# A gated recurrent layer: the order of three engines written out, and the side sums moved to other products

## The chip, the cores and the metric

The kernel runs on one core of one Trainium2 chip. The metric is the time of one execution on the device in microseconds (us), here the median of three runs. A core has a matrix engine (TensorE, PE in the profile, its weight loads PEld), an engine for elementwise work (VectorE, DVE), one for functions and copies (ScalarE, ACT), GpSimd (POOL), and a queue engine (SyncE, SP) that issues most DMAs. Each engine works through its own instructions in order and waits for others by semaphores.

## The reference

Two post-norm decoder layers on a sequence of 1024 positions and width 1024, in float32: a dilated attention layer with an MLP, then a gated recurrent layer (HGRN2, eight heads of 128) with an MLP. The change is in the recurrent layer:

```python
q_raw, f_raw, i_raw = jnp.split(x @ w_in, [H * K, 2 * H * K], axis=-1)
log_f = jnp.logaddexp(jnp.log(lb), jnp.log1p(-lb) + jax.nn.log_sigmoid(z))
key = (1.0 - lb) * jax.nn.sigmoid(-z)          # z is f_raw
q = jax.nn.silu(q_raw)
b = jnp.cumsum(log_f, axis=3)                  # within chunks of 64
a = jnp.where(causal, einsum(q * exp(b), key * exp(-b)), 0.0)
kv = einsum(key * exp(b_last - b), v)
state = exp(b_last) * state + kv               # from chunk to chunk
o = a @ v + (q * exp(b)) @ state_before
o = o * rsqrt(mean(o * o) + eps) * norm_g
y = o @ w_out
...
return jnp.square(jax.nn.relu(x @ w_up)) @ w_down     # the MLP
```

## The kernel before

**Products.** Large products are cut into 2 x 2 blocks and made with seven block products instead of eight (numbers 1 to 7 in the code, in an order such as 1, 6, 2, 7, 5, 4, 3). Each operand is split into a high and a low half (`split`: a ScalarE copy, then a VectorE subtraction), and a block product of the gated layer is 4 x 3 = 12 matmuls of 128 x 512. Several block products of one tile add up in one PSUM bank, so the next may start only when the bank has been copied or added out.

**Side sums.** Four of the seven products need sums of weight blocks. For the gated layer they are made ahead, by a generator (`Gates.sums`) that is advanced one step at a time beside the MLP of layer 0. A step is one VectorE instruction on 128 x 512, in half of the steps with a ScalarE copy behind it. GpSimd's queue writes the results to DRAM (`gwd`), and SyncE's loads them back as `H`. There are twelve units of eight steps. In the up-projection `SIDE_UP` gives steps per product, in the down-projection `SIDE_DOWN` steps per step by number of product, and the rest runs in the gated layer.

**The gated layer** (`hgrn`). A table `gw.seq` lists the block products: 28 for the values (`values`, bank tiles "pvx" and "pvy"), seven gate products for each head (`gate`, tile "pg"; numbers 1, 2, 6, 3 give z and the forget gate, 5, 7, 4 the query). Then each head has small pieces: `forget` and `query` (ScalarE functions Abs, Exp, Ln with VectorE passes between), transposes of the keys ("hpt" to "k2n"), products of keys and values ("kvps"), the running states ("stA", "stB", fifteen VectorE updates), the product of queries and keys ("as", masked into "aT"), the outputs ("ho"), their squares and scaling ("sq", "rms", "on") and the transposes back ("opt" to "oN"). In the kernel before, `head_pieces` gives them as seven lists, one of which is emitted after each gate product. The order in which an engine takes them is then left to the scheduler.

**The out-projection** (`outproj_ln`, tile "pmm") begins with three tiles over six heads. `pre` loads and splits the first `NPRE` heads' rows before it. Pieces of the last heads are emitted between its matmuls.

`in_order` ties the instructions of the engines it is given to the order in which they are written, by dependences without a semaphore. The up-projection uses it for TensorE, VectorE and SyncE; the gated layer did not use it.

## Time and profile before

| | |
|---|---|
| median of 3 runs | 2710.69 us (2709.29 to 2713.7) |
| the profiled execution | 2713.53 us, granted TensorE clock 0.996 |
| its span | 2711.8 us |
| value products, first to last | 1659.9 to 1775.6 us |
| gate products, first to last | 1694.4 to 1978.6 us |
| out-projection of the gated layer | 1986.8 to 2089.5 us |

The span runs from the first to the last instruction. A row of a group of instructions names the source line, the engine, the operation, the tile written and the tiles read, the shape and the count; behind the bar stand busy time, mean ns of one, then the idle time of the engine before them and what ended it. A busy TensorE is a union of overlapping matmuls, so its real pace is read from the count of matmuls in a window.

### The profile page before, as it was taken

To read this page: it belongs to the slowest core of one execution; us is meant where nothing else is said; L and a number is where in the kernel's file an instruction comes from. 1 tells how busy PE (TensorE), PEld (TensorE's weight loads), DVE (VectorE), ACT (ScalarE), POOL (GpSimd) and SP (SyncE) were. 2 spreads that over 40 slices of the span, in tenths; PEclk is the share of its full clock that TensorE was granted. 3 is DMA by queue.
4 is the path that set the end of the run, shared out by engine and by line. 5 is a ranking of instruction groups with operands and counts; after the bars stand their busy time and mean duration, and the time that the engine had idled before them with its cause. 6 is when DMAs were issued, how large, how long until landed. Compare 5 with 4: busy or idle time off the path is not lost.

```text
span 2711.8 us, 41759 instructions
## 1 busy us (share of the span) xinstructions
PE 2654.8 (98%) x14600; PEld 2171.6 (80%) x14600; DVE 2109.3 (78%) x4053; ACT 1420.0 (52%) x3169; POOL 216.5 (8%) x424
## 2 busy tenths in 40 slices
PE   8999999999999999999999999999989999999998
PEld 6888888888887778877788887777778888888887
DVE  7768878778788788888787988557778786678686
ACT  5556555555655626445553546446653644444443
POOL 1021222212132100000000000000000000000000
PEclk9999999999999999999999999999999999999999
DMA  8677778777789634577895962754443464486653
GB/s 326 211 243 227 225 205 238 225 229 230 242 263 308 206 98 174 204 251 270 304 337 163 370 212 86 258 195 138 154 131 121 153 224 159 162 298 235 225 181 122
DMA packets 240899, 583.30 MB, mean 215 GB/s; under 512 B 29488, under 2 KB 51248, under 8 KB 240688
## 3 DMA queue, kind: packets, MB, share of 16 engines
q1 hardware_dynamic: 213584, 503.06, 54.6%
q0 software_dynamic: 27104, 77.58, 9.4%
q8 instruction: 115, 1.88, 0.3%
q14 instruction: 96, 0.79, 0.1%
HBM read 429.44 MB, written 125.89 MB: 205 GB/s over the span
## 4 chain that ended last, share of the span: by engine, by line
PE 82%; DVE 8%; ACT 4%; DMA 3%; issue 2%; SPq 0%; DVEq 0%; POOL 0%; ACTq 0%
PE pmm L816 8%; PE pmm L818 7%; PE pmm L817 7%; PE pup L1369 6%; PE pup L1371 6%; PE pup L1370 6%; PE pdy L1519 4%; PE pdy L1520 4%; PE pdy L1516 4%; PE pdx L1519 3%; PE pdx L1520 3%; PE pdx L1516 3%; PE pmm L217 2%; PE o L691 2%; PE pmm L218 2%
## 5 line engine op out<-in xcount | busy, mean ns | idle before, releaser
L816 PE MATMUL pmm<-xh,H 128*128 128x512 f32 x1008 | 403.2, 400 | 8.1 <-ACT H L522 6.4
L818 PE MATMUL pmm<-xh,H 128*128 128x512 f32 x1008 | 395.8, 393 | 4.2 <-DVE H L531 4.0
L817 PE MATMUL pmm<-xl,H 128*128 128x512 f32 x1008 | 395.3, 392 | 4.0 <-DVE xl L172 4.0
L816 PEld LDWEIGHTS pmm<-xh,H 128*128 128x128 f32 x1008 | 190.7, 189 | 57.4 <-issue 8.6
L818 PEld LDWEIGHTS pmm<-xh,H 128*128 128x128 f32 x1008 | 190.6, 189 | 46.9 <-DVE H L531 5.9
L817 PEld LDWEIGHTS pmm<-xl,H 128*128 128x128 f32 x1008 | 190.8, 189 | 42.2 <-DVE xl L172 4.6
L1516 PE MATMUL pdy<-dT,dS 128*128 128x512 f32 x512 | 199.2, 389 | 0.0
L1519 PE MATMUL pdy<-dT,dS 128*128 128x512 f32 x512 | 199.2, 389 | 0.0
L1520 PE MATMUL pdy<-dT,dS 128*128 128x512 f32 x512 | 199.2, 389 | 0.0
L171 ACT ACTIVATE dS<-dr 128x512 fp32r<-128x512 f32 x192 | 119.2, 621 | 56.1 <-PE pdy L1520 23.8
L172 DVE TENSOR_TENSOR dS<-dr,dS 128x512 fp32r<-128x512 f32 x192 | 131.1, 683 | 16.4 <-ACT dS L171 15.8
L630 ACT ACTIVATE p<-p,stats 128x256 f32<-128x256 f32 (+1 forms) x256 | 118.2, 465 | 48.9 <-DVE stats L627 48.3
L627 DVE CUSTOM_DVE_ANT_0 p<-s,mask 128x256 f32<-128x256 f32 (+1 forms) x256 | 82.4, 376 | 47.5 <-PE s L599 47.5
L171 ACT ACTIVATE dT<-dr 128x512 fp32r<-128x512 f32 x128 | 79.2, 624 | 71.9 <-DVE dr L1489 38.3
L1330 ACT ACTIVATE H<-wc 128x512 fp32r<-128x512 f32 x128 | 77.5, 624 | 73.9 <-DVE wc L1323 40.6
L1516 PEld LDWEIGHTS pdy<-dT,dS 128*128 128x128 f32 x512 | 96.1, 188 | 20.0
L1519 PEld LDWEIGHTS pdy<-dT,dS 128*128 128x128 f32 x512 | 96.1, 188 | 20.0
L1520 PEld LDWEIGHTS pdy<-dT,dS 128*128 128x128 f32 x512 | 96.1, 188 | 19.8
L891 POOL DMA_DIRECT2D rot<-e x176 | 85.8, 493 | 281.6 <-ACT e L849 62.2
L1519 PE MATMUL pdx<-dT,dS 128*128 128x512 f32 x256 | 99.7, 389 | 0.7 <-DVE dT L172 0.7
L1520 PE MATMUL pdx<-dT,dS 128*128 128x512 f32 x256 | 99.4, 389 | 0.0
L1516 PE MATMUL pdx<-dT,dS 128*128 128x512 f32 x256 | 98.4, 389 | 0.0
(534 smaller groups left out, 7040.2 us busy)
## 6 DMA issues: line engine op xcount, KB each, us to landing
xh<-xtd SPq DMA_DIRECT2D x116, 512.0 KB, 6.9
xl<-xtd SPq DMA_DIRECT2D x116, 512.0 KB, 5.8
dr<-hd SPq DMA_DIRECT2D x192, 256.0 KB, 5.0
dr<-in_w_down_dram SPq DMA_DIRECT2D x160, 256.0 KB, 5.3
wa<-in_w_up_dram SPq DMA_DIRECT2D x48, 512.0 KB, 3.9
gwd<-pH POOLq DMA_DIRECT2D x48, 512.0 KB, 6.5
H<-gwd SPq DMA_DIRECT2D x48, 512.0 KB, 5.5
rot<-e POOLq DMA_DIRECT2D x176, 128.0 KB, 6.4
```

Source lines behind the costliest of these rows:

```text
L171: act(hi, raw, AF.Copy)
L172: nc.vector.tensor_sub(lo, raw, hi.bitcast(F32))
L630: act(p[:, h], p[:, h], AF.Exp, bias=self.sS[:, 0, h, b:b + 1], scale=-1.0, accum_out=self.sS[:, 1, h, b:b + 1])
L816: nc.tensor.matmul(o, wh, hi[k // 2][:, c], start=begin and k == 0, stop=False, skip_group_check=True)
L817: nc.tensor.matmul(o, wh, lo[k // 2][:, c], start=False, stop=False, skip_group_check=True)
L818: nc.tensor.matmul(o, wl, hi[k // 2][:, c], start=False, stop=end and k == 3, skip_group_check=True)
L1369: nc.tensor.matmul(o, wh, xf.h(b, k), start=begin and k == 0, stop=False, skip_group_check=True)
L1370: nc.tensor.matmul(o, wh, xf.l(b, k), start=False, stop=False, skip_group_check=True)
L1371: nc.tensor.matmul(o, wl, xf.h(b, k), start=False, stop=end and k == 3, skip_group_check=True)
L1516: nc.tensor.matmul(o[q], h, T_[:, L], start=begin, stop=False, skip_group_check=True)
L1519: nc.tensor.matmul(o[q], h, T_[:, R], start=False, stop=False, skip_group_check=True)
L1520: nc.tensor.matmul(o[q], l, T_[:, L], start=False, stop=end, skip_group_check=True)
```

## The change

The pieces of a head become fifteen methods of a class `Head`, and a table puts each of them behind a numbered product: the pieces of head h begin at `first[h] + 3`, beside its own gate products, and end at `first[h] + 15`, in the second head after it. Everything in the layer is written inside `in_order` for TensorE, VectorE and ScalarE.

```diff
-        heads = {}
+        first = {h: gw.seq.index(("g", h, 1)) for h in range(1, 8)}
+        first[0] = first[1] - 7
...
+        for h in range(8):
+            w = Head(h)
+            s0 = first[h]
+            g, q = (...) if h == 0 else (s0 + 3, s0 + 6)
+            for n, f in enumerate((w.forget0, w.forget1, w.forget2, w.forget3)):
+                at(g + n, f)
+            at(q, w.query0)
+            at(g + 3, w.forget4)
+            at(q + 1, w.query1)
+            at(s0 + 7, w.values)
+            at(s0 + 8, w.trans)
+            at(q + 2, w.query2)
+            at(s0 + 9, w.kv)
+            at(s0 + 9, lambda w=w: w.states(0))
+            at(s0 + 10, lambda w=w: w.states(1))
+            at(s0 + 10, w.amat)
+            at(s0 + 11, w.masked)
+            at(s0 + 12, w.omats)
+            at(s0 + 13, w.squares)
+            at(s0 + 14, w.scaled)
+            at(s0 + 15, w.outs)
+        rank = {"scaled": 0, "outs": 2}
+        order = in_order((mybir.EngineType.PE, mybir.EngineType.DVE, mybir.EngineType.Activation))
...
+            for f in sorted(fill.pop(n, []), key=lambda f: rank.get(f.__name__, 1)):
+                f()
+            for k in range(n + 2, n + 6):
+                if k < len(gw.seq) and k <= n + gw.lead(k):
+                    gw.split(k)
+            if 15 < n < first[1] or n >= first[1] and (n - first[1]) % 7 in (0, 2, 6):
+                next(gw.side, None)
+            k = n - first[7]
+            if 0 <= k < 3:
+                pre(oN, k, 0)
+            if 3 <= k + 0 < 6:
+                pre(oN, k - 3, 1)
```

The values' products change places with gate products, the sums get other places, one more head's rows are split ahead of the out-projection, and banks change: "as" goes to the bank "o", "opt" to "o" and "s", which "kvps" and "ho" use too.

```diff
-NPRE = 2
+NPRE = 3
-SIDE_UP = (0.25, 0.96)
-SIDE_DOWN = {5: 0.9, 4: 0.25, 2: 0.25}
+SIDE_UP = {(1, 2): 2, (1, 7): 1, (1, 5): 2, (2, 2): 2, (2, 7): 1, (2, 5): 2}
+SIDE_DOWN = {5: 0.95, 4: 0.4, 2: 0.3}
...
-            self.seq = v[0] + v[1] + [("g", h, i) for h, i in ((0, 2), (0, 1), (1, 2), (2, 2), (0, 5), (0, 6), (0, 3), (0, 7))]
-            self.seq += v[2][:1] + [("g", 0, 4)] + v[2][1:] + v[3] + v[4] + v[5] + v[6]
+            self.seq = v[0] + [("g", 0, 2), ("g", 1, 2)] + v[1]
+            self.seq += [("g", h, i) for h, i in ((0, 1), (2, 2), (0, 5), (0, 6), (0, 3), (0, 7))]
+            self.seq += v[2] + [("g", 0, 4)] + v[3] + v[4] + v[5] + v[6]
...
-            t = self.raw[e] = wp.tile([P, 512], F32, name="wr", tag="p")
+            t = self.raw[e] = U("wr")[:, 0:512] if 3 < n < 16 else wp.tile([P, 512], F32, name="wr", tag="p")
...
+        def lead(self, k):
+            e = self.seq[k]
+            return 0 if e is None else {1: 5, 2: 4, 4: 5}.get(e[2], 0) if e[0] == "g" and k > 20 else 2
...
-                a = bank("s", "as")
+                a = self.am = bank("o", "as")
...
-                pt = bank("pt", "opt")
+                    pt = bank("s" if j else "o", "opt")
```

In heads 6 and 7 the sixth product of a head (number 2 of the head after next) does not exist; the table then holds `None` there, and the slot has no matmuls.

What the change moves is best seen on three places. The first is ScalarE in the middle of the heads. Before, from the squares "sq" of one head to the Exp of "ze" of the next; "a_..." are the tiles a1 and a3 of the forget gate and the query, "qe" and "ze" the query and z:

```order
L1946 ACTIVATE sq,rms<-ho 128x128 x6
L2090 ACTIVATE dec<-a_18192 128x16
L1946 ACTIVATE sq,rms<-ho 128x128 x2
L2055 ACTIVATE ze<-pg 128x512
L2085 ACTIVATE ls<-ze,hc_C 128x1024
L1948 ACTIVATE rms<-rms 128x8
L1949 ACTIVATE rms<-rms 128x8
L2067 ACTIVATE qe<-pg 128x512
L2088 ACTIVATE ze<-ze,hc_C 128x1024
```

And ScalarE there now:

```order
L2120 ACTIVATE qe<-pg 128x512
L2005 ACTIVATE sq,rms<-ho 128x128 x8
L2007 ACTIVATE rms<-rms 128x8
L2008 ACTIVATE rms<-rms 128x8
L1916 ACTIVATE ls<-ze,hc_C 128x1024
L1918 ACTIVATE dec<-a_18477 128x16
L1925 ACTIVATE a_18589<-qe 128x1024
L1928 ACTIVATE ze<-ze,hc_C 128x1024
L1932 ACTIVATE a_18589<-a_18589 128x1024
L1933 ACTIVATE a_18589<-a_18589,one 128x1024
L2112 ACTIVATE qe<-pg 128x512
L1948 ACTIVATE k2n<-hpt 128x512 x2
```

The copy of the head's last gate product ("qe<-pg") stood behind the squares and stands ahead of them now; the Exp of "ze", on which the transposes "hpt" wait, follows the squares and the Abs of the query.

The second is VectorE from the scaled outputs "on" to the first states, at the same place of a head. Before:

```order
L1956 TENSOR_TENSOR on<-ho,rms 128x512 x2
L2057 TENSOR_TENSOR ze<-pg,ze 128x512
L2099 SCALAR_TENSOR_TENSOR a_18048<-qe,a_18048 128x1024
L2100 TENSOR_TENSOR a_18048<-a_18048,a_17911 128x1024
L2102 TENSOR_TENSOR qe<-qe,a_18048 128x1024
L1915 COPY stA<-kvps 128x128
```

Now, with a step of the side sums ("pH<-ps,pH") and two splits of gate weights ("H<-wr,H") between them:

```order
L2110 TENSOR_TENSOR ze<-pg,ze 128x512
L2012 TENSOR_TENSOR rms<-rms 128x8
L2013 TENSOR_TENSOR rms<-rms 128x8
L2014 TENSOR_SCALAR rms<-rms 128x8
L2015 TENSOR_TENSOR rms<-rms 128x8
L2019 TENSOR_TENSOR on<-ho,rms 128x512 x2
L1934 SCALAR_TENSOR_TENSOR a_18016<-qe,a_18016 128x1024
L1935 TENSOR_TENSOR a_18016<-a_18016,a_17902 128x1024
L1801 TENSOR_TENSOR pH<-ps,pH 128x512
L1939 TENSOR_TENSOR qe<-qe,a_18016 128x1024
L171 TENSOR_TENSOR H<-wr,H 128x512 x2
L1976 COPY stA<-kvps 128x128
```

The addition "ze<-pg,ze" moved ahead of the scaling, and three more instructions stand ahead of the states.

The third is VectorE in the up-projection of layer 0, from one product 6 ("upb<-pup,upa") to product 5 of the same pair. The sums' steps are the rows with "ps" and "pH". Before:

```order
L1384 TENSOR_TENSOR upb<-pup,upa 128x512
L1338 TENSOR_TENSOR H<-wc_12407,H 128x512
L1411 TENSOR_TENSOR upb<-upc,upa 128x512
L1796 TENSOR_TENSOR pH<-ps,pH 128x512
L1338 TENSOR_TENSOR H<-wc_12357,H 128x512
L1411 TENSOR_TENSOR upa<-upb 128x512
L1804 TENSOR_TENSOR ps<-pa,pb 128x512
L1387 TENSOR_TENSOR upc<-pup,upa 128x512
L1338 TENSOR_TENSOR H<-wb,H 128x512
L1808 TENSOR_TENSOR ps<-ps,pa 128x512
L1393 TENSOR_TENSOR upc<-pup,upc 128x512
```

And now:

```order
L1389 TENSOR_TENSOR upb<-pup,upa 128x512
L1343 TENSOR_TENSOR H<-wc_12363,H 128x512
L1416 TENSOR_TENSOR upb<-upc,upa 128x512
L1343 TENSOR_TENSOR H<-wc_12318,H 128x512
L1416 TENSOR_TENSOR upa<-upb 128x512
L1813 TENSOR_TENSOR ps<-ps,pa 128x512
L1801 TENSOR_TENSOR pH<-ps,pH 128x512
L1392 TENSOR_TENSOR upc<-pup,upa 128x512
L1343 TENSOR_TENSOR H<-wb,H 128x512
L1821 TENSOR_TENSOR ps<-pa 128x512
L1398 TENSOR_TENSOR upc<-pup,upc 128x512
```

The step beside product 6 is gone; beside product 2 there are two.

## The prediction

> **What bounds the kernel now.** The page comes first: the span, the busy shares and the chain of waits.

> ```profile
> span 2711.8 us, 41759 instructions
> PE 2654.8 (98%) x14600; PEld 2171.6 (80%) x14600; DVE 2109.3 (78%) x4053; ACT 1420.0 (52%) x3169; POOL 216.5 (8%) x424
> PE 82%; DVE 8%; ACT 4%; DMA 3%; issue 2%; SPq 0%; DVEq 0%; POOL 0%; ACTq 0%
> ```

> TensorE sets the time: it is idle for 2711.8 - 2654.8 = 57 us, and the change gives it the same products to do. So the change can only move TensorE's waits, and I look for them by stage, in the view of windows (columns: window, its length, then busy us and count of PE, PEld, DVE, ACT, POOL; granted TensorE clock; DMA). The first two windows hold the same 1143 matmuls, those of the up-projection from its seventeenth block product on, in layer 0 (where the side sums for the gated layer run) and in layer 1 (where none run). Then come the values, the heads, and the hand-over to the out-projection.

> ```profile
> 1079.08:1349.28 270.20, 266.97 (x1143) 211.21 (x1142) 216.76 (x347) 142.16 (x245) 14.94 (x28) 1.00 0.73 254
> 2134.65:2393.68 259.03, 259.03 (x1143) 214.34 (x1142) 186.66 (x296) 125.41 (x217) 0.00 (x0) 1.00 0.51 179
> 1659.90:1775.80 115.90, 112.12 (x499) 91.45 (x498) 74.48 (x134) 47.11 (x95) 4.26 (x8) 0.99 0.60 219
> 1775.80:1978.80 203.00, 189.01 (x1537) 152.50 (x1536) 145.26 (x253) 130.15 (x266) 0.00 (x0) 1.00 0.45 153
> 1978.80:2030.00 51.20, 44.24 (x287) 35.36 (x287) 37.99 (x72) 28.59 (x68) 0.00 (x0) 0.90 0.34 108
> ```

> The up-projection of layer 0 takes 270.20 - 259.03 = 11.2 us more than its twin. Idle time shows only 3.2 of that; the rest is matmuls that start late after short waits. A matmul of 512 columns costs 259.03 / 1143 = 0.227 us, so a gate product of twelve takes 2.72. Who is waited for, in TensorE's waits of the up-projection (first two rows) and of the gated layer:

> ```profile
> PE pup L1369 <- DVE upb L1384: 1.5, 4, 0.5
> PE pup L1369 <- ACT upa L1374: 1.0, 2, 0.5
> ...
> PE opt L1964 <- DVE on L1956: 15.2, 7, 6.8
> PE as L1897 <- DVE stB L1917: 3.0, 6, 0.7
> PE kvps L1909 <- DMA vn<-vald: 2.5, 1, 2.5
> PE pvx L2008 <- ACT vp L2015: 2.0, 1, 2.0
> PE pvy L2008 <- DVE vu L2020: 1.7, 1, 1.7
> ```

> **The change, part by part.**

> *Side sums in the up-projection.* Layer 0 has 347 - 296 = 51 more VectorE instructions than its twin, the sums', and they cost 11.2 us. They now stand only beside products 2, 7 and 5 of a pair, five steps in seven products where it was 0.96 a product, and none beside the first forty of this window, where it was one in four. VectorE's own work beside products 1 and 4 is four instructions of 0.6 us, as long as the product; a fifth there is what makes "upb" and "upa" late, and it goes. No slot now holds more than four. About 37 of the 51 steps stay, so by count alone 27% of 11.2, that is 3.1 us, goes; all of it would be 11.2. I take 9.5, near the upper end, as the waits named stand at the crowded slots alone. The steps that leave run in the down-projection (four more), where VectorE has room, in the values (one more), and 21 beside the heads.

> *Values.* Two gate products, 24 x 0.227 = 5.4 us, now stand between value products 1 and 2, where TensorE waited 2.0 us for the copies "vp". One, 2.7 us, stands between products 6 and 7, where it waited 1.7 us for "vu". Both covers are longer than the waits. The first wait cost more than itself:

> ```profile
> 1677.30:1680.71 3.41, 1.40 (x8) 0.98 (x7) 3.41 (x9) 2.79 (x7) 0.00 (x0) 1.00 0.01 3
> 1680.71:1684.12 3.41, 3.41 (x10) 2.62 (x8) 3.41 (x8) 3.41 (x10) 0.00 (x0) 0.50 0.42 154
> ```

> The clock was 0.50 for the next 3.41 us, 1.7 us lost. So 2.0 + 1.7 + 1.7, together 5.4; I take 5, bounds 3 (ScalarE, now in written order behind the layer norm's copies, still late) to 5.4.

> *Heads.* This is where the order is written out, and I lay one head out from rows of one head of before (first TensorE from the timeline, then groups of ScalarE and VectorE).

> ```profile
> 1868.43 1.25 PE L1964 MATMUL opt<-ident,on 128*128 128x128 f32 x8 [1.52 <-DVE on L1956]
> 1884.84 1.15 PE L1897 MATMUL as<-qe,ls 128*64 128x64 f32 x32 [0.48 <-DVE stB L1917]
> 1898.37 1.25 PE L1964 MATMUL opt<-ident,on 128*128 128x128 f32 x8 [1.52 <-DVE on L1956]
> ...
> L1909 PE MATMUL kvps<-vn,k2n 64*128 64x128 f32 x30 | 2.0, 279 | 0.0
> L1889 PE MATMUL hpt<-ident,ze 128*128 128x128 f32 x8 | 1.0, 272 | 0.0
> ```

> A head takes 29.94 us (1868.43 to 1898.37) with 2.0 of idle, some 2.3 with the restarts, so 27.6 are work.

> ```profile
> L2067 ACT ACTIVATE qe<-pg 128x512 f32<-128x512 f32 x1 | 0.6, 580 | 0.0
> L1946 ACT ACTIVATE sq<-ho 128x128 f32<-128x128 f32 x8 | 2.1, 270 | 0.0
> L1949 ACT ACTIVATE rms<-rms 128x8 f32<-128x8 f32 x1 | 0.2, 209 | 0.0
> L2085 ACT ACTIVATE ls<-ze,hc_C 128x1024 f32<-128x1024 f32 x1 | 1.2, 1152 | 0.0
> L2088 ACT ACTIVATE ze<-ze,hc_C 128x1024 f32<-128x1024 f32 x2 | 2.3, 1148 | 0.9 <-DVE ze L2087 0.9
> L2098 ACT ACTIVATE a<-a,one 128x1024 f32<-128x1024 f32 x1 | 1.2, 1152 | 0.0
> L2101 ACT ACTIVATE a<-a 128x1024 f32<-128x1024 f32 x1 | 1.1, 1058 | 1.1 <-DVE a L2100 1.1
> L1965 ACT ACTIVATE oN<-opt,hg 128x512 f32<-128x512 f32 x2 | 1.3, 688 | 1.1 <-PE opt L1964 1.1
> ```

> ```profile
> L2087 DVE TENSOR_TENSOR ze<-a,ze 128x1024 f32<-128x1024 f32 x1 | 1.2, 1225 | 1.1 <-ACT ls L2085 1.1
> L2099 DVE SCALAR_TENSOR_TENSOR a<-qe,a 128x1024 f32<-128x1024 f32 x1 | 1.2, 1224 | 2.6 <-ACT a L2098 2.6
> L172 DVE TENSOR_TENSOR H<-wr,H 128x512 fp32r<-128x512 f32 x3 | 2.1, 686 | 0.0
> L1917 DVE SCALAR_TENSOR_TENSOR stA<-stA,dec,kvps 128x128 f32<-128x128 f32 x6 | 2.1, 348 | 0.3
> L1899 DVE COPY_PREDICATED aT<-cm,as 128x512 f32<-128x512 uint8 x1 | 0.7, 748 | 0.3 <-PE as L1897 0.3
> ```

> Zero is the end of a head's last gate product. ScalarE may not start the squares before its copy of that product: copy to 0.8, squares to 2.8, the two tiny ones with VectorE's step between them to 3.4, Exp of "ls" to 4.6. VectorE subtracts to 5.8, ScalarE takes Exp of "ze" to 7.0: only now can "hpt" run, and TensorE's two gate products ended at 5.4. On ScalarE follow Exp and Ln of "a3" to 9.1; VectorE's two passes to 11.6 (it blocks there, with the sums and H halves behind it); ScalarE's Exp to 12.7 and the two copies "oN" to 13.9. The second copy frees the bank that the odd half of "kvps" needs, so "kvps" ends near 14.9. TensorE has 3 x 2.72 + 2.0 for "kvps" + about 1.9 for sixteen transposes = 12.1 to do until then, so it waits 2.75, against 2.3 before: the wait for "on" is only spread over three places. After that VectorE has the multiplication to 13.9, two H halves to 15.7, eight states to 18.7, three half-tiles to 20.5, seven states to 23.0, a half-tile and the mask to 24.3; TensorE reaches "ho" with slots 3, 4, 5 and "as" at 24.3. No slack, but no wait. So heads 2 to 5 lose 0.4 each. Heads 6 and 7 have no product in slot 5 to cover the mask: without sums and one H half it is ready near 23.1, TensorE near 21.6, so 1.5 more in head 6 and, with the out-projection's splits among VectorE's work, 2.5 in head 7. Together 6.5 slower; bounds 14 faster (all idle of that window, 203.00 - 189.01) to 12 slower (1.5 more a head). The 2.5 for "vn" stays: "kvps" is asked for as early as before, and the stores are no earlier.

> *Hand-over.* Before, TensorE idled 6.8 us for head 6's "on", 51.20 - 44.24 = 7.0 in all. The clock of 0.90 means 0.10 x 51.20 = 5.1 us of clock lost, half of it while it idled anyway: 2.6 more, together 9.6. Now 27 matmuls of the out-projection on heads 0 to 2, which are split ahead, stand before that "opt", 6.1 us. But VectorE still owes both heads' pieces and eighteen splits of 0.6 us there, as many as before, so I count 3.5 won, bounds 0 and 9.6.

> Sum: 9.5 + 5 - 6.5 + 3.5 = 11.5 us faster. The profiled execution took 2713.53 us (1.7 outside the span), 2.8 above the median of 2710.69. So 2702 in its own terms, and 2710.69 - 11.5 = 2699, rounded to 2700, against the median.

> **A rule weighed.** A head's transposes and waits now stand together, from 5.4 to 9.7 with no gate product. Do transposes keep the clock up? Four rows: the value window above without its transposes, a window in the heads, the one after it, and that in the heads without its transposes.

> ```profile
> 1677.30:1680.71 3.41, 0.96 (x4) 0.48 (x3) 0.00 (x0) 0.95 (x2) 1.00 0.01 3
> ...
> 1926.47:1929.88 3.41, 1.89 (x13) 1.31 (x12) 2.17 (x7) 2.03 (x3) 0.00 (x0) 1.00 0.00 0
> 1929.88:1933.29 3.41, 3.41 (x21) 2.90 (x20) 0.69 (x1) 3.35 (x4) 0.00 (x0) 1.00 0.62 182
> ...
> 1926.47:1929.88 3.41, 0.88 (x5) 0.49 (x3) 0.00 (x0) 0.00 (x0) 1.00 0.00 0
> ```

> In the head the products alone were busy 0.88 us of 3.41, less than the 0.96 that led to half clock, and yet the next window ran at 1.00; with the transposes it is 1.89 against 1.40. So here transposes count. [...]

> **The rivals.** *Half clock in the heads.* If that gap trips the clock in six heads, 6 x 1.7 = 10 us go: 2710. One such window in six would not surprise; all of them need transposes not to count. 6%. [...]

> *The sums still collide.* If only the count matters, the up-projection gives 3.1 instead of 9.5: 2706. For it: VectorE keeps 37 of 51. Against: the waits stand at crowded slots. 10%.

> *The written order removes the heads' waits.* If squares and Exp overlap better than I laid out, the 6.5 go and up to 14 of idle with them: near 2680. Against: the stretch to 13.9 is nearly all ScalarE and VectorE work in line. 10%.

> *Slower: VectorE's fixed queue becomes the heads' bound.* From slot 3 on it has no slack, so any late instruction (a sum that waits for its load, an H half) is paid in full, once a head. 1.6 us a head, over seven heads, eats the 11.5; at 3 it is 2720. For it: 21 sums are now in that queue, and nothing can pass them. Against: loads are issued some slots ahead. 14%.

> **How the numbers follow.** The forecast has 60%; its own range is 2691 to 2709 by the bounds above. The range over cases goes from 2686 to 2713 and leaves out most of the third and fourth rival. A measurement of this kernel tells about 0.2%, 5.4 us, from no change. Faster by more: 55 of the forecast's 60, the third rival's 10, 2 of the second's: 67%. Within it: 5 of the forecast, 8 of the second, the first's 6: 19%. Slower: 14%.

> **What would show it.** The twin window of the up-projection should fall from 270 to about 261; the values should lose both waits and the half clock; a head's period should be 30 to 30.5, with TensorE waiting for "ze", "on" and the copy "oN" instead of "on" and "stB". A period under 29 or over 31.5 would prove the layout wrong, a clock of 0.5 inside the heads the reading of the transposes.

## The result and the profile after

The changed kernel takes 2752.86 us (median of 4 runs, 2751.49 to 2753.87) against 2711.57 for the kernel before on the same chip: ratio 1.0152, 95% interval 1.0134 to 1.017. It is 41 us slower where 11 us faster was forecast. First the page of the changed kernel: span, busy times and chain.

```profile
span 2752.1 us, 41764 instructions
PE 2665.7 (97%) x14600; PEld 2185.4 (79%) x14600; DVE 2111.7 (77%) x4053; ACT 1422.8 (52%) x3169; POOL 216.4 (8%) x424
PE 30%; ACT 2%; DVE 2%; DMA 1%; issue 0%; SPq 0%; DVEq 0%; ACTq 0%
```

The work is the same; TensorE is idle for 2752.1 - 2665.7 = 86 us, where it was 57. The chain this time covers only 35% of the span, so it locates nothing. By stage, in the view of windows with the columns as before: the 1143 matmuls of the up-projection, the values, the heads up to the last gate product, the hand-over.

```profile
1078.55:1348.44 269.89, 263.40 (x1143) 215.30 (x1141) 207.95 (x331) 135.06 (x234) 10.09 (x19) 0.99 0.65 226
1658.28:1797.69 139.41, 120.30 (x498) 95.62 (x497) 77.82 (x138) 49.81 (x96) 5.33 (x10) 0.91 0.53 186
1797.69:2021.70 224.01, 197.04 (x1544) 158.90 (x1543) 157.03 (x272) 136.50 (x270) 4.26 (x8) 0.96 0.51 173
2021.70:2075.00 53.30, 47.02 (x302) 37.23 (x301) 36.73 (x69) 27.80 (x74) 0.00 (x0) 0.97 0.27 89
```

The up-projection kept its time, 269.9 for 270.2, with 16 VectorE instructions fewer. From first to last value matmul it is 139.4 for 115.7, at a mean clock of 0.91. The heads take 224.0 for 203.0. TensorE's waits over the whole program (waits in total, times, longest):

```profile
PE hpt L1947 <- ACT ze L1928: 9.1, 7, 1.5
PE pvx L2062 <- ACT H L170: 8.5, 2, 4.2
PE kvps L1968 <- DMA vn<-vald: 8.4, 1, 8.4
PE pg L2104 <- ACT H L170: 7.6, 2, 5.5
...
PE pup L1374 <- ACT H L1335: 6.2, 2, 5.4
...
PE kvps L1968 <- ACT oN L2030: 2.2, 3, 0.7
```

Two of them, "hpt" for "ze" and "kvps" for "oN", were forecast. New are the splits "H" in the values (16.1 us in four waits), one wait of 5.4 in the up-projection, and "vn", 8.4 where it was 2.5. The two waits that the values had before, for "vp" and "vu", are gone, as forecast.

**The values.** ScalarE beside them, from the timeline:

```profile
1687.11 0.60 ACT L2108 ACTIVATE ze<-pg 128x512 f32<-128x512 f32 x1 [2.52 <-PE pg L2106]
1687.98 0.38 ACT L267 ACTIVATE f0n22h<-lnpt 128x256 fp32r<-128x256 f32 x1 [0.28 <-PE lnpt L257]
1688.86 0.38 ACT L267 ACTIVATE f0n22h<-lnpt 128x256 fp32r<-128x256 f32 x1 [0.49 <-DVE f0n22l L268]
1689.14 0.59 ACT L331 ACTIVATE fs<-lnpt 128x512 f32<-128x512 f32 x1
1690.49 0.72 ACT L267 ACTIVATE f0nT3h<-fs 128x256 fp32r<-128x256 f32 x2 [0.76 <-DVE fs L332]
1691.12 0.71 ACT L267 ACTIVATE f0nT1h<-fs 128x256 fp32r<-128x256 f32 x2
1692.36 0.72 ACT L267 ACTIVATE f0nT2h<-fs 128x256 fp32r<-128x256 f32 x2 [0.54 <-DVE fs L335]
1693.63 0.72 ACT L267 ACTIVATE f0nT4h<-fs 128x256 fp32r<-128x256 f32 x2 [0.55 <-DVE fs L337]
1694.26 0.61 ACT L170 ACTIVATE H<-wr 128x512 fp32r<-128x512 f32 x1
```

Rows 2 to 8 are one piece of the layer norm (`late.pop(0)()`): from the end of the copy "ze" at 1687.71 to 1694.26 it waits once for TensorE's transposes ("lnpt") and then goes to and fro between ScalarE and VectorE. The split "H<-wr" of the next weights (last row) is written behind it and starts when it ends. TensorE's next product starts at 1694.92, after 4.2 us of waiting, and the granted clock was 0.50 from 1693.05 to 1699.87. ScalarE was not full in that time; it was waiting in a fixed order.

**The up-projection.** VectorE in the timeline:

```profile
1198.75 0.69 DVE L1416 TENSOR_TENSOR upa<-upb 128x512 f32<-128x512 f32 x1
1207.87 0.69 DVE L1809 TENSOR_TENSOR ps<-pb 128x512 f32<-128x512 f32 x1 [8.44 <-DMA pb<-in_w_hgrn_dram]
1208.48 0.69 DVE L1392 TENSOR_TENSOR upc<-pup,upa 128x512 f32<-128x512 f32 x1
```

SyncE issued that load at 1201.73. Product 2 of the first pair has two steps: the generator's first step only loads, and the second, right behind it, uses what was loaded. VectorE stood for 8.4 us with its in-order queue behind it, TensorE for 5.4, and the granted clock was 0.50 for 6.8 us behind it (1208.35 to 1215.18).

**The load of "vn".** DMA issues around the last value products (KB each, median us to landing), before and then after:

```profile
vald<-vu SPq DMA_DIRECT2D x4, 256.0 KB, 6.5
vn<-vald SPq DMA_DIRECT2D x1, 512.0 KB, 4.0
```

```profile
vald<-vu SPq DMA_DIRECT2D x4, 256.0 KB, 9.6
wr<-in_w_hgrn_dram SPq DMA_DIRECT2D x3, 256.0 KB, 6.2
pa<-in_w_hgrn_dram SPq DMA_DIRECT2D x1, 512.0 KB, 7.5
gwd<-pH POOLq DMA_DIRECT2D x1, 512.0 KB, 8.8
pb<-in_w_hgrn_dram SPq DMA_DIRECT2D x1, 512.0 KB, 10.2
vn<-vald SPq DMA_DIRECT2D x1, 512.0 KB, 5.0
```

The values' last stores land after 9.6 us instead of 6.5, and "vn" is read only then: its load is issued at 1810.45, right behind the last landing. Loads and a store of the side sums ("pa", "pb", "gwd") now run beside these stores; the DMA engines moved 5.3 MB in these 15 us and were busy throughout, against 3.5 MB and 74% in the 13 us shown of the kernel before. That the sums' transfers alone stretch the stores is not shown: in e11 below, with "pa", "pb" and three stores of the sums among the issues from 1755 to 1775, these four land after 5.5.

### The profile page after: what moved, and what is told of

It is laid out like the page before. It is cut to its first block, busy times and chain, and to the rows that moved or that the text cites. A ratio compares the mean times of both kernels' runs of the same rounds, so it can differ in the third digit from the quotient of the medians.

```text
span 2752.1 us, 41764 instructions
## 1 busy us (share of the span) xinstructions
PE 2665.7 (97%) x14600; PEld 2185.4 (79%) x14600; DVE 2111.7 (77%) x4053; ACT 1422.8 (52%) x3169; POOL 216.4 (8%) x424
## 5 line engine op out<-in xcount | busy, mean ns | idle before, releaser
L1524 PEld LDWEIGHTS pdy<-dT,dS 128*128 128x128 f32 x512 | 96.2, 188 | 19.8
```

The lines of the kernel that those rows point to most:

```text
L1524: nc.tensor.matmul(o[q], h, T_[:, R], start=False, stop=False, skip_group_check=True)
```

## Experiments

All times are medians; the ratios are to the kernel before, run beside each group. The three stage lengths are those of the one profiled execution of each run. Executions of one kernel lie up to 11 us apart, and e1, e2, e7, e9, e14 and e16 have two each, so a difference of a few us between two medians is not read. "Stretch" is the time of the 1143 matmuls of the up-projection, "values" from their first to their last matmul, "heads" from there to the last gate product.

| | stretch | values | heads | median us | ratio (95%) |
|---|---|---|---|---|---|
| before | 270.2 | 115.7 | 203.0 | 2711.6 | |
| the change | 269.9 | 139.4 | 224.0 | 2752.9 | 1.0152 (1.0134 to 1.017) |
| e1 splits first | 267.5 | 132.6 | 224.3 | 2742.5 | 1.012 (1.0099 to 1.0141) |
| e2 load early | 259.6 | 144.0 | 220.7 | 2742.4 | 1.012 (1.0099 to 1.014) |
| e3 before, sums alone | 259.6 | 118.6 | 208.9 | 2713.1 | 1.0011 (1.0001 to 1.002) |
| e4 no order | 267.3 | 123.6 | 203.4 | 2713.4 | 1.0013 (1.0003 to 1.0024) |
| e5 e2, values free | 259.6 | 116.9 | 223.7 | 2720.6 | 1.0046 (1.0033 to 1.0059) |
| e6 e2, all free | 260.1 | 118.5 | 206.5 | 2700.8 | 0.9965 (0.9955 to 0.9974) |
| e7 e5, z first | 259.6 | 118.9 | 226.9 | 2725.8 | 1.0059 (1.0039 to 1.0079) |
| e9 e2, ScalarE's order alone | 259.5 | 131.8 | 217.3 | 2728.7 | 1.007 (1.005 to 1.009) |
| e14 e2, late pieces loose | 259.6 | 134.8 | 220.8 | 2732.5 | 1.008 (1.006 to 1.0101) |
| e11 e6, one gate product later | 259.6 | 114.7 | 210.1 | 2701.4 | 0.9964 (0.9951 to 0.9977) |
| e12 e11, sums in the down-projection | 259.6 | 114.7 | 196.7 | 2689.5 | 0.992 (0.9904 to 0.9937) |
| e16 e2, sums in the down-projection | 260.5 | 138.9 | 215.1 | 2732.2 | 1.0083 (1.0062 to 1.0103) |
| e19 e16, values free | 259.6 | 117.4 | 213.7 | 2710.6 | 1.0005 (0.9994 to 1.0015) |
| e17 e3, sums in the down-projection | 260.3 | 114.3 | 207.0 | 2702.3 | 0.9974 (0.9962 to 0.9985) |

**Splits ahead of the layer norm's pieces.**

```diff
             elif e:
                 gate(*e[1:])
+            for k in range(n + 2, n + 6):
+                if n < 16 and k < len(gw.seq) and k <= n + gw.lead(k):
+                    gw.split(k)
             if late and n % 2 == 0:
```

> The changed kernel, but in the first sixteen products of the gated layer the weight splits are written ahead of the layer norm's pieces instead of behind them. Theory (written order): TensorE's waits for the splits H (5.5, 4.2, 4.2 us and half clock behind them) go, the values take 116 to 120 us from first to last product instead of 139.4, and the time falls by about 20, to 2733. Rival (the new order of the products, or late loads of the weights, make the splits late): the values stay at 139 and the time at 2753.

Values 132.6: 6.8 of the 23.7 lost are back. The direction is the theory's, the size is not. The first wait was still 3.8 us: its split stood behind the copies of a value product, and these behind the layer norm's piece ahead of them.

**The first load four products earlier.**

```diff
+            beside(side and n == 2 * NAHEAD + 38)
             beside(SIDE_UP.get(...
```

> The changed kernel, but the side sums are begun four products earlier: their first step, which only loads, stands at the second last product before the first pair and no longer directly ahead of the first addition. Theory (the one stall of 5.6 us and the half clock behind it are the first load, 6.7 us on its way, on which VectorE waits in written order): the stretch of 1143 matmuls of the up-projection falls from 269.9 to about 261, and the time by 9, to 2744. Rival (side sums still collide with the crowded slots): the stretch stays within 2 us of 269.9.

```profile
1077.50:1337.10 259.60, 259.60 (x1143) 214.07 (x1142) 208.07 (x332) 136.34 (x236) 10.15 (x19) 1.00 0.69 237
```

The stretch falls by 10.3, to within 0.6 of the twin in layer 1 (259.03), TensorE busy throughout with 332 VectorE instructions against the twin's 296. So the sums do fit at those products, and nearly the whole gain of their new places had been spent on one load. The values are 4.6 longer here than in the change, with one more wait for a split (3.5), and the heads 3.3 shorter ("vn" 5.0 for 8.4); why was not followed up.

**The new places of the sums alone, in the kernel before.** `SIDE_UP` and `SIDE_DOWN` and the early load as above, the load of each next unit two steps earlier in the generator, as the change has it too, and steps beside three gate products of a head:

```diff
                 gate(a, b)
+                if n > 34 and b in (1, 6, 4):
+                    next(gw.side, None)
```

> The kernel before with only the new places of the side sums in the up- and down-projection, begun four products earlier, and with steps beside three gate products of a head for those that are left. Theory (the waits came from crowded slots): the stretch of 1143 matmuls falls from 270.2 to about 261 and the time from 2711 to about 2702. Rival (only the number of steps counts): about 267 and 2708. Second rival (the steps beside the heads cost there what is won): the stretch 261, the time 2711.

The second rival came true: the stretch gives 10.6, and the values (2.9), the heads (5.9) and the end of the out-projection take it back. The steps that leave the up-projection are not free where they go.

**No written order in the gated layer.**

```diff
-        order = in_order((mybir.EngineType.PE, mybir.EngineType.DVE, mybir.EngineType.Activation))
+        order = in_order(())
```

> The changed kernel, with the same code and the same places in it, but no written order in the gated layer: the scheduler orders TensorE, VectorE and ScalarE there. Theory (the written order of ScalarE holds the splits up): the values take about 120 us instead of 139.4, and the time is 2725 to 2740; the heads may change either way. Rival (the places in the code, the products' new order or the banks cost the time): the values stay near 139 and the time near 2753.

39 us come back at one line, with the same pieces, places, products and banks: more than expected, as the heads gain too (203.4 for 224.0). In the values 15.8 of the 23.7 come back, and TensorE's waits for ScalarE's splits fall from 16.1 to 5.1.

**Order in the heads only; none, with the early load; ScalarE's alone.** `order.__enter__()` at `n == first[1]`; `in_order(())`; `in_order((mybir.EngineType.Activation,))`, all with e2's early load.

> The changed kernel with the early load of the sums (as in the run before), and the written order begun only at the first gate product of head 1: the values and the gate products between them are the scheduler's, the heads stay in written order. Theory (the written order costs its time in the values): values 124 us as without any order, heads with the period of 30.3 that they have now, time 2742 - 20 = 2722. Rival (the order of the heads costs most of it): values still above 135, or the time above 2735.

> The changed kernel with the early load of the sums and no written order in the gated layer. If the two causes add up, 2713.4 - 8 to 10 = 2703 to 2706: faster than the kernel before by 0.2%. Rival: the up-projection's gain is lost in the values and the heads, as in the kernel before with the new places of the sums (2713): then 2711 to 2715.

> The changed kernel with the early load of the sums, and the written order in the gated layer for ScalarE alone; TensorE and VectorE are the scheduler's. Theory (ScalarE's order holds the splits up): the values take 135 to 145 us, as with all three engines in order. Rival (VectorE's or TensorE's order does it): about 124.

With the early load the full order costs 2742.4 - 2700.8 = 41.6. Freeing the values alone gives 21.8, freeing the heads the other 19.8. ScalarE's order alone costs 2728.7 - 2700.8 = 27.9 and brings 13 of the 25.5 us in the values (131.8 - 118.5 of 144.0 - 118.5); it came out at 131.8, under the range of 135 to 145, so the other two engines' order adds the rest. e6 is faster than the kernel before, by 9 us, though not in the values: 118.5 for 115.7. Even without the order they keep new waits for splits (1.9 for ScalarE's part, 3.0 for VectorE's).

**The layer norm's pieces alone exempt from the order.**

```diff
-        order = in_order((mybir.EngineType.PE, mybir.EngineType.DVE, mybir.EngineType.Activation))
+        loose = set()
+        order = in_order((mybir.EngineType.PE, mybir.EngineType.DVE, mybir.EngineType.Activation), loose)
...
             if late and n % 2 == 0:
+                mark = len(nc.cur_bb.bb.instructions)
                 late.pop(0)()
+                loose.update(i.name for i in list(nc.cur_bb.bb.instructions)[mark:])
```

> The changed kernel with the early load of the sums and everything in the gated layer in written order, except the instructions of the layer norm's pieces (f0.., fs, lnpt), which the scheduler may place. Theory (it is these pieces, a chain that goes to and fro between ScalarE, VectorE and TensorE, that hold up the splits written behind them): the values fall from 144 to 118 to 122 us, the heads stay at 220, the time is near 2742 - 23 = 2719, as with the values wholly free (2720.6). Rival (the rest of the written order, such as the splits behind the copies of a value product or behind the Exp of ze, holds them as much): values above 130, time above 2730.

The values fall by 9.2, to 134.8, not to 120: the rival holds for the larger part. One more thing that holds a split up is seen on ScalarE in this run:

```profile
1758.86 0.63 ACT L1799 ACTIVATE pH<-ps 128x512 fp32r<-128x512 f32 x1 [7.83 <-DMA gwd<-pH]
1759.39 0.61 ACT L170 ACTIVATE H<-wr 128x512 fp32r<-128x512 f32 x1
```

A copy of the side sums waits 7.8 us for a store to free its buffer, the split behind it waits with it, and TensorE waits 4.2 us for the split. In the changed kernel one such copy stood for 10.4 us until 1809.72, for "vald<-vu".

**The chain of z ahead of the squares.**

```diff
-        rank = {"scaled": 0, "outs": 2}
+        rank = {"scaled": 0, "forget3": 0, "query0": 2, "outs": 2, "query2": 3}
```

> As e5_values_free (heads alone in written order), but in a head's seventh slot the Exp of ls stands ahead of the squares and the Abs of the query behind the Exp of ze, and in its ninth slot the copies oN ahead of the query's last Exp. Theory (hpt waits 1.5 us for ze because the squares stand ahead of its chain, kvps 0.75 for the copies oN): hpt waits 0.7 or less, kvps not at all, the heads' period falls from 30.3 to 28.0 to 28.8, and the time by 9 to 14 against e5. Rival (VectorE's fixed queue has no room): as or ho wait for VectorE instead, the period stays above 29.5.

```profile
PE kvps L1969 <- DMA vn<-vald: 9.7, 1, 9.7
PE ho L1993 <- DVE aT L1959: 7.3, 5, 3.0
...
PE hpt L1948 <- ACT ze L1929: 3.0, 6, 0.9
```

The rival came true. "hpt" waits 3.0 in six heads instead of 8.9, the wait for "oN" is gone, and "ho" now waits 7.3 for the mask "aT" (2.0 in e5), which VectorE reaches too late. What was won on ScalarE was lost again on VectorE.

**A gate product behind the values, and the sums in the down-projection**, both without written order and with the early load.

```diff
-SIDE_DOWN = {5: 0.95, 4: 0.4, 2: 0.3}
+SIDE_DOWN = {5: 1, 4: 1, 2: 0.5}
...
-            self.seq += [("g", h, i) for h, i in ((0, 1), (2, 2), (0, 5), (0, 6), (0, 3), (0, 7))]
-            self.seq += v[2] + [("g", 0, 4)] + v[3] + v[4] + v[5] + v[6]
+            self.seq += [("g", h, i) for h, i in ((0, 1), (0, 5), (0, 6), (0, 3), (0, 7))]
+            self.seq += v[2] + [("g", 0, 4)] + v[3] + v[4] + v[5] + v[6] + [("g", 2, 2)]
```

> As e6_free_load_early (no written order, early load), with the gate product 2 of head 2 moved from between the values to behind the last of them. Theory (the first kvps waits 7 us for vn because too little work stands between the last value product and it): that wait falls by the product's 2.7, part of the half clock behind it goes, and the time falls by 2 to 4, to 2697 to 2699. Rival (the load is late for its queue's sake and slides with the rest, or the products between the values lack a cover): the wait stays at 6 to 8 or comes up among the values; time 2700 to 2703.

> As e11_one_gate_later, with a step of the side sums beside every product 5 and 4 and every second product 2 of the down-projection, so that fewer, or none, run beside the values and heads. Theory (their loads and stores crowd the queues just where the values are stored and vn is read): the wait for vn falls to 2 to 4, the heads gain a little, and the time is 2690 to 2696; the down-projection stays at 309.6. Rival (VectorE is full there): the down-projection grows by 4 or more and the time is 2700 or above.

The second edit alone is e11, both are e12. e11 shortens the wait for "vn" from 7.0 to 4.8 and gains nothing, as 1.8 us of waiting for "vu" come up at the first gate product behind the values. The wait for "vn" has another source here than in the change. In e11 SyncE's queue stands for 5.5 us ahead of a load of "H", until a store of the side sums has landed, and the values' last four stores stand behind it; in e6 it stands for 3.5 in the same way, ahead of a load "pb". The row of e11:

```profile
SPq L1846 <- DMA gwd<-pH: 5.5, 1, 5.5
```

The first of the four is issued at 1769.71, 8.8 us after the end of the last value matmul (5.5 in e6). In e12 that wait is gone, and the first is issued 0.8 before that end. The heads of e11, and then of e12:

```profile
1760.50:1970.60 210.10, 195.91 (x1549) 159.14 (x1549) 154.50 (x273) 132.91 (x268) 4.26 (x8) 0.98 0.53 181
```

```profile
1761.60:1958.30 196.70, 191.63 (x1550) 155.66 (x1549) 145.78 (x256) 129.21 (x261) 0.00 (x0) 1.00 0.48 161
```

All fourteen steps of the side sums and their eight stores by GpSimd are gone from the heads, and with them 13.4 us. The down-projection has 40 steps for 25 and takes 0.6 more (310.2 for 309.6); the values keep 17 of 19. The wait for "vn" goes altogether. The period of the heads in the middle is the same in both, 28.9; some 12 of the 13.4 lie ahead of the second head's "hpt", where "vn" is waited for. e12 is 11.9 us faster than e11: the best version here, 0.8% under the kernel before. TensorE's longest waits from the values into the out-projection:

```profile
PE hpt L1948 <- ACT ze L1929: 5.9, 6, 1.9
PE pg L2105 <- ACT H L170: 1.9, 1, 1.9
PE pg L2107 <- DVE H L171: 1.7, 1, 1.7
```

**Order and sums apart.** The fuller `SIDE_DOWN` with the written order (e16), with the order in the heads alone (e19), and in the kernel before with e3's edits (e17).

> The changed kernel in written order throughout, with the early load and with a step of the side sums beside every product 5 and 4 and every second product 2 of the down-projection, so that hardly any is left for the values and heads. Theory (order and crowded queues are two causes): the first kvps waits 3 us or less for vn, the waits for H<-gwd among the values go, but the splits stay late: values 128 to 140 instead of 144, and the time 2712 to 2725. Rival (without the sums the written order costs little): values under 122, time under 2705.

> As e16_order_sums_down, with the written order begun only at the first gate product of head 1. Theory (the order of the heads by itself costs what their period shows, 30.3 against 28.7 without order, 1.6 in seven heads): values 115 to 117, 205 to 209 us from the last value to the last gate product against 197 without order, time 2698 to 2703. Rival (without sums in it VectorE's fixed queue has room, and the period falls to the scheduler's): 197 to 200 us, time 2690 to 2693.

> The kernel before with the new places of the side sums, the early load and the fuller down-projection; the heads' pieces, products and banks as before. Theory (the places of the sums are most of what the best version has, the fifteen pieces without order give the heads 1 to 1.5 us a head): up-projection 259.6, values 114 to 116, heads 200 to 203, time 2695 to 2699. Rival (the pieces give nothing): 2690, as e12; second rival (the pieces are the larger part): 2705 or more.

Without sums beside the heads the written order costs as much as with them: freeing the values gives 21.7 (e16 to e19), and e12 is another 21.1 faster than e19, with one product elsewhere, a move that was worth nothing between e6 and e11. e16 came out slower than either theory had it: values near the upper end, and "vn" waited for 4.1 us and not 3. In e16 and e19 four heads in a row have the same period of 30.3, with the same two waits (1.5 for "ze", 0.75 for "oN"); in e12 it is 28.9. e19 too is slower than expected: its heads take 17.0 more than e12's, though e12's hold one gate product (2.7) more. Of these 19.7 the period explains some 9, the wait for "vn" 3.4 and those for the mask in the last heads 2.0; the rest is open. e17 shows what the new places of the sums give without the rest of the change: 2702.3, or 8.1 under the kernel before. So the pieces, products and banks, left to the scheduler, are worth another 12.7 (2702.25 - 2689.51); they were not tested apart.

## Why the prediction was wrong

By stage, forecast and then measured (us won): up-projection 9.5 and 0.3, values 5 and -23.7, heads -6.5 and -21.0, hand-over 3.5 and 2.7. The measured ones add up to 41.7 lost, for 41.3 in the medians.

The step that failed most is the one on the **values**: 5 us won, with the bound "3 (ScalarE, now in written order behind the layer norm's copies, still late)". It named what is ahead of the copies and asked only how much of an old wait would remain. It did not lay out the order of ScalarE there as it did for a head, and so never saw that the splits now stood behind a piece of 6.5 us, with only one product of 2.7 us on TensorE as cover. Measured: 23.7 slower; e4 and e5 show the order as the main cause (15.8 of the 23.7 in e4; with the early load, 25.5 of 28.3 between e2 and e6). e1 and e14 show that the layer norm's pieces are 7 to 9 us of it; the rest is shared by copies of products and of side sums ahead of the splits and by the two other engines, and was not taken apart further. Nor would the 5 have come without the order: the two old waits went, as forecast, and the scheduler's values were still 2.8 longer than before (e6).

**Up-projection:** the reading of the collisions was right and sized well (9.5 forecast, 10.6 in e2 and e3). The sum missed one thing: a step counted as an instruction is in its first instance a load, and two steps stand together at product 2. That cost 10.4 (2752.9 to 2742.4). The count of steps was off too: 17 left the up-projection, 4 of them for the values and 14 for the heads, and the down-projection got one fewer, where 1, 21 and four more were forecast.

**Heads:** 6.5 slower was forecast, with a period of 30 to 30.5 and waits for "ze", "on" and "oN". The waits came, and the period where nothing else fell into a head: four times in a row in e16 and e19. In the changed kernel itself the five periods from the second head's "hpt" to the seventh's are 31.4, 33.9, 30.9, 30.3 and 29.2. One head of it:

```profile
1968.27 1.09 PE L1947 MATMUL hpt<-ident,ze 128*128 128x128 f32 x8 [1.48 <-ACT ze L1928]
1969.20 1.15 PE L2029 MATMUL opt<-ident,on 128*128 128x128 f32 x8
...
1973.04 1.38 PE L1968 MATMUL kvps<-vn,k2n 64*128 64x128 f32 x18
1975.16 0.94 PE L1968 MATMUL kvps<-vn,k2n 64*128 64x128 f32 x12 [0.75 <-ACT oN L2030]
```

The period is 30.32 from this head's "hpt" back to the one before, the two waits 2.2, against 2.75 in the layout. What made it 21 was outside the layout: "the 2.5 for vn stays" was wrong (8.4, 5.9 more), the mean clock was 0.96 (PE busy 197.0 for 189.0), and one "kvps" waited 2.0 for "k2n". And the comparison hid a larger loss: with the same pieces the scheduler makes a head in 28.9 (e12), so the written order costs 1.4 a head against what the change could have had.

**Hand-over:** from the last gate product to the last matmul of the out-projection 108.2 for 110.9, 2.7 won where 3.5 was forecast. **Down-projection:** no loss, as forecast, though with one step fewer; e12 shows that it has room for more (40 steps for 25 in 0.6 us more).

**Rivals:** the slower one named VectorE's fixed queue in the heads; the largest loss was ScalarE's in the values, for the same reason (in the written order nothing passed an instruction that waited: ScalarE's 6.5 us beside the values, VectorE's 8.4 in the up-projection). e7 shows that VectorE's queue has no slack either (7.3 us of waiting for the mask). A clock of 0.50 came in three windows behind the wait for "vn" (1809.10 to 1819.34) and in two in the middle of heads (from 1843.23 and from 1880.78), not in every head. The prediction named a clock of 0.5 inside the heads as a sign that its reading of the transposes was wrong; the last section shows that this reading holds, and that the two windows were short of work with the transposes counted.

The parts, in us, along a chain of runs: new places of the sums, with those that leave the up-projection in the down-projection, -8.1 (before to e17); pieces, products and banks -12.7 (to e12); sums beside the heads instead of the down-projection +11.9 (to e11); one gate product back among the values -0.6 (to e6); written order +41.6 (to e2); the late first load +10.4 (to the change). A chain adds up by itself, so the sum, +42.5, proves nothing; it differs from the measured 41.3 by what the kernel before differed between two groups of runs (2710.4 and 2711.6). Each part was measured with the others in one particular state, and has another size elsewhere: without the early load the order costs 39.4.

## What to carry to other kernels

An order written out over several engines must be laid out for every stage that it covers, not only for the one that it was made for: follow each instruction that TensorE waits for back to what stands ahead of it on its queue and ask what that one waits for. Where work is moved in steps, look at what the first step does (here a load) and give it its latency. Work taken out of a crowded stage goes where both the engine and the DMA queues have room: the same fifteen or so steps cost 12 us around the last values and in the heads, and 0.6 us in the down-projection (310.2 for 309.6, e12 and e11).

## What the runs showed of the hardware

```profile
1839.82:1843.23 3.41, 1.62 (x11) 0.96 (x9) 3.27 (x9) 3.19 (x4) 0.00 (x0) 1.00 0.93 303
1870.54:1873.95 3.41, 1.93 (x13) 1.39 (x12) 3.06 (x8) 3.19 (x6) 0.00 (x0) 1.00 1.01 340
1877.37:1880.78 3.41, 1.45 (x7) 0.91 (x6) 1.57 (x2) 1.81 (x4) 0.00 (x0) 1.00 0.00 0
```

```profile
1208.35:1211.76 3.41, 1.96 (x5) 1.53 (x6) 2.71 (x5) 1.80 (x4) 0.00 (x0) 0.50 0.00 0
```

The windows after the first and the third ran at 0.50, the one after the second at 1.00: 1.62 and 1.45 us of work lost the full clock, 1.93 kept it. The edge is not sharp: over the change's trace, the least that kept it was 1.63 (the window from 2024.14) and the most that lost it 1.69 (from 1744.25). At half clock 1.96 was not enough to get the full clock back: the window after the fourth ran at 0.50 again.

Transposes counted as work in these traces. In the change, one window in the heads and the one after it, with all instructions, then the first without its transposes (by the tile "pg"):

```profile
1966.11:1969.53 3.42, 1.94 (x14) 1.45 (x14) 3.28 (x8) 3.16 (x4) 0.00 (x0) 1.00 0.00 0
1969.53:1972.94 3.41, 3.41 (x19) 2.62 (x17) 2.56 (x3) 2.31 (x5) 0.00 (x0) 1.00 0.00 0
```

```profile
1966.11:1969.53 3.42, 0.68 (x3) 0.21 (x2) 0.68 (x1) 0.00 (x0) 1.00 0.00 0
```

The products alone were busy for 0.68 us, and the next window ran at 1.00; the window from 1744.25 had 1.69 us and no transpose, and the next ran at 0.50. So in this kernel transposes count, as in the prediction's four rows.

Behind the first load's stall matmuls of 512 columns start every 0.43 us at 0.50 (from 1212.10) and every 0.23 at 1.00 (from 1215.60). By these two numbers a window at 0.50 with TensorE busy throughout costs some 1.6 us, an estimate. In the change such a stretch held one window (behind 1744.25), two (the first load's stall) or three (the wait for "vn").
